# Rotary part of the attention scores as two fp32r products with query and key split into high and low parts

## The chip, the cores and the metric

The kernel runs on one core of a Trainium2 chip. The metric is the device time of one launch in microseconds (us), the median of the runs. The engines of the core are TensorE (PE for its matmuls, PEld for its weight loads), VectorE (DVE), ScalarE (ACT), GpSimd (POOL) and the queue of SyncE (SP), which issues nearly all transfers. Each engine works through its own list of instructions in the order in which the build put them there.

## The reference

One decoder layer: a feed-forward half step, a mixing step in which a gated recurrence (HGRN2) and multi-head latent attention stand beside one another, another feed-forward half step, a gated embedding and a last norm; 512 positions, width 1024. The part that matters is the attention's score, a sum of a part without position (128 columns a head) and a rotary part (64 columns, whose key is the same for all four heads):

```python
q = (rms_norm(cq, q_a_norm[i]) @ w_q_up[i]).reshape(B, S, MLA_HEADS, QK_DIM)
q_nope, q_rope = jnp.split(q, [NOPE_DIM], axis=-1)            # 128 and 64 columns
q_rope = apply_rope(q_rope, cos[:, :, None, :], sin[:, :, None, :])
k_rope = apply_rope(kr, cos, sin)                             # one key for all heads
qf = jnp.concatenate([q_nope, q_rope], axis=-1)
kf = jnp.concatenate([k_nope, k_rope broadcast over the heads], axis=-1)
s = einsum('bhqd,bhkd->bhqk', q[:, :, lo:hi], k[:, :, :hi]) * scale   # 128 queries, keys up to them
```

## The kernel before

Large matmuls run as three fp32r products: each operand is split into a high part (ScalarE copies it to the type fp32r) and a low part (VectorE subtracts the high part from it), and `mm3` adds high·high, high·low and low·high (lines 226 to 230). Products on activations, the attention's scores among them, run as plain fp32, which the trace shows as two matmul instructions each.

Weights come in pieces of 512 KB through seven raw buffers; SP issues a load (line 63) as soon as VectorE has made the low part of the piece whose buffer it takes (lines 73 and 74 make the parts).

Before the attention, `up_projections` makes for each head the queries `qn`, then for each pair of heads the raw rotary queries `qr` in a PSUM bank (heads one above the other, 64 rows each), then four keys `kn`, then four value blocks `vm`. All of these products go through the three PSUM banks with the tag `acc`, in turn, so a bank is taken again by the third next product and must have been copied out by then: `kn` by VectorE (line 826), `qn` and `vm` by ScalarE.

`rope` (line 670) rotates a pair of heads: ScalarE copies the bank to `rpa`, four DMAs on SP's queue bring its rows, with halves exchanged, to `rpb`, VectorE multiplies `rpa` by the cosines and `rpb` by the sines, and two additions of 64 rows each write the two heads' `qr`. Each `qr` has 128 rows, half of them zeros that GpSimd set long before (line 818). The rotary key `krope` holds the 64 key rows twice, one above the other, so that a head's rows meet the key and the other half of the product adds zeros.

`attend` (line 846) takes, for each head, four blocks of 128 queries with 128, 256, 384 and 512 keys: a score bank is the sum of an fp32 product of `kn` and `qn` (line 852) and one of `krope` and `qr` (line 853). Mask, maximum, exponential, normalisation, transposes and the product with `vm` (line 875) follow. `weave` puts steps of the values' projection `uv` and of the recurrence's output `oh` between these steps.

Code order is not the whole order: the framework schedules the instructions of each engine when the kernel is built, and what stands in an engine's list is then fixed.

Of the kernel before, what the change touches and what calls it, by code (L numbers as in the profile page):

```python
# [10 lines left out]
F32 = mybir.dt.float32  # L11
F32R = mybir.dt.float32r
I32 = mybir.dt.int32
U8 = mybir.dt.uint8
AF = mybir.ActivationFunctionType
ALU = mybir.AluOpType
# [147 lines left out]
def block_kernel(ctx: ExitStack, tc: tile.TileContext, xT, pT, pos, wst, items, vecs, lnf, cmask, tmask, out):  # L164
    nc = tc.nc
    V, S, G, PE = nc.vector, nc.scalar, nc.gpsimd, nc.tensor
# [9 lines left out]
    def nm(s):  # L176
        count[0] += 1
        return f"{s}_{count[0]}"

    def slot(name, dt=F32):  # L180
        return slots.tile([P, T], dt, tag="slot", name=nm(name), bufs=NSLOT)
# [50 lines left out]
    def split(src, hi, lo, g=None):  # L232

        if g is None:
            S.activation(hi, src, AF.Copy)  # L235
            V.tensor_tensor(lo, src, hi.bitcast(F32), op=ALU.subtract)  # L236
        else:
            S.activation(hi, src, AF.Copy, scale=g)
            V.scalar_tensor_tensor(lo, src, g, hi.bitcast(F32), op0=ALU.mult, op1=ALU.subtract)
# [373 lines left out]
    kvs = {}  # L613

    def lora():

        us = [acc("uc") for _ in range(3)] + [tps("uc")]
        for k in range(KD):
            w_hi, w_lo = W.next(4)
            for tb in range(4):  # L620
                ts = slice(tb * P, (tb + 1) * P)
                mm3(us[tb][:, :448], (nmix.hi[k][:, ts], nmix.lo[k][:, ts]), (w_hi[:, :448], w_lo[:, :448]),
                    k == 0, k == KD - 1)
                if tb % 2:
                    yield
        kr = slot("kr").rearrange("p (j w) -> p j w", j=4)
        cs = [slot("c") for _ in range(4)]
        ss = tmp.tile([P, 8], F32, tag="css", name="css", bufs=1)
        for tb in range(4):
            S.activation(cs[tb][:, :384], us[tb][:, :384], AF.Copy, scale=rc[:, tb:tb + 1])  # L630
            S.activation(kr[:, tb, :64], us[tb][:, 384:448], AF.Copy, scale=rc[:, tb:tb + 1])
        for tb in range(4):
            sq = tmpt("sq", tag="sq", bufs=2)
            S.activation(sq[:, :256], cs[tb][:, :256], AF.Square, accum_out=ss[:, tb:tb + 1])
            S.activation(sq[:, 256:384], cs[tb][:, 256:384], AF.Square, accum_out=ss[:, 4 + tb:5 + tb])
        yield
        r = rsqrt_of(ss, 8, (256, 128))
        for tb in range(4):
            V.tensor_scalar(cs[tb][:, :256], cs[tb][:, :256], r[:, tb:tb + 1], None, op0=ALU.mult)
            V.tensor_scalar(cs[tb][:, 256:384], cs[tb][:, 256:384], r[:, 4 + tb:5 + tb], None, op0=ALU.mult)  # L640
        yield
        for j, gcol in enumerate((V_QAN, V_QAN + 1, V_KVAN)):
            tp = aux("cT")
            for tb in range(4):
                PE.transpose(tp[:, tb * P:(tb + 1) * P], cs[tb][:, j * P:(j + 1) * P], ident)
            hi, lo = slot("ch", F32R), slot("cl", F32R)
            split(tp, hi, lo, vcol(gcol))
            xc.append((hi, lo))
            yield
        tp = aux("csT")  # L650
        for i, t in enumerate((cos, sin)):
            for tb in range(4):
                o = (i * 4 + tb) * 64
                PE.transpose(tp[:, o:o + 64], t[:64, tb * P:(tb + 1) * P], ident[:64, :64])
        a, b = (tmpt("kra").rearrange("p (j w) -> p j w", j=4) for _ in range(2))
        c4, s4 = (tp[:, i * 256:(i + 1) * 256].rearrange("p (j w) -> p j w", j=4) for i in range(2))
        V.tensor_tensor(a[:, :, :64], kr[:, :, :64], c4, op=ALU.mult)
        for i in range(2):
            o, n = slice(i * 32, (i + 1) * 32), slice(32 - i * 32, 64 - i * 32)
            V.tensor_tensor(b[:, :, o], kr[:, :, n], s4[:, :, o], op=ALU.mult)  # L660
        for i in range(2):
            V.tensor_tensor(kr[:, :, i * 64:(i + 1) * 64], a[:, :, :64], b[:, :, :64], op=ALU.add)
        tp = aux("krT")
        for tb in range(4):
            PE.transpose(tp[:, tb * P:(tb + 1) * P], kr[:, tb, :], ident)
        kvs["rope"] = slot("krope")
        S.activation(kvs["rope"], tp, AF.Copy)
        yield

    def rope(u, outs):  # L670

        a, b = tmpt("rpa"), tmpt("rpb")
        S.activation(a, u, AF.Copy)
        for s in range(4):
            d = s ^ 1
            nc.sync.dma_start(b[d * 32:(d + 1) * 32, :], a[s * 32:(s + 1) * 32, :])
        V.tensor_tensor(a, a, cos, op=ALU.mult)
        V.tensor_tensor(b, b, sin, op=ALU.mult)
        for i, t in enumerate(outs):
            rows = slice(i * 64, i * 64 + 64)  # L680
            V.tensor_tensor(t[rows], a[rows], b[rows], op=ALU.add)

    def chain(*gens):
        for g in gens:
# [116 lines left out]
    qn, qr, kn, vm = [], [], [], []  # L801

    def up_projections():
        for hd in range(H):
            u = acc("qn")
            for j in range(2):
                mm3(u, W.next(), xc[j], j == 0, j == 1)
            t = slot("qn")
            S.activation(t, u, AF.Copy)
            qn.append(t)  # L810
            yield
        for pr in range(2):
            u = acc("qr")
            for j in range(2):
                mm3(u, W.next(), xc[j], j == 0, j == 1)
            ts = [slot("qr") for _ in range(2)]
            for i, t in enumerate(ts):
                G.memset(t[64 - i * 64:128 - i * 64], 0.0)
            rope(u, ts)
            qr.extend(ts)  # L820
            yield
        for hd in range(H):
            u = acc("kn")
            mm3(u, W.next(), xc[2], True, True)
            t = slot("kn")
            V.tensor_copy(t, u)
            kn.append(t)
            yield
        w = W.next(4)
        for j in range(4):  # L830
            u = acc("vm")
            ts = slice(j * P, (j + 1) * P)
            mm3(u, (xc[2][0][:, ts], xc[2][1][:, ts]), w, True, True)
            t = slot("vm")
            S.activation(t, u, AF.Copy)
            vm.append(t)
            yield
# [3 lines left out]
    krope = kvs["rope"]  # L841
# [4 lines left out]
    def attend(hd):  # L846
        pt = [slot("pt") for _ in range(4)]
        for i in range(4):
            n = (i + 1) * P
            qs_ = slice(i * P, n)  # L850
            s = tps("sc")
            PE.matmul(s[:, :n], qn[hd][:, qs_], kn[hd][:, :n], start=True, stop=False)
            PE.matmul(s[:, :n], qr[hd][:, qs_], krope[:, :n], start=False, stop=True)
            V.tensor_tensor(s[:, qs_], s[:, qs_], cm, op=ALU.add)
            mxr = tmp.tile([P, 1], F32, tag="mx", name=nm("mx"), bufs=4)
            V.reduce_max(mxr, s[:, :n], axis=mybir.AxisListType.X)
            V.tensor_scalar(mxr, mxr, -QK_SCALE, None, op0=ALU.mult)
            pr = slot("pr")
            sm = tmp.tile([P, 1], F32, tag="sm", name=nm("sm"), bufs=4)
            S.activation(pr[:, :n], s[:, :n], AF.Exp, bias=mxr, scale=QK_SCALE, accum_out=sm)  # L860
            V.reciprocal(sm, sm)
            V.tensor_scalar(pr[:, :n], pr[:, :n], sm, None, op0=ALU.mult)
            yield
            tp = aux("tp")
            for j in range(i + 1):
                PE.transpose(tp[:, j * P:(j + 1) * P], pr[:, j * P:(j + 1) * P], ident)
            for j in range(i + 1):
                if j % 2:
                    V.tensor_copy(pt[j][:, qs_], tp[:, j * P:(j + 1) * P])
                else:  # L870
                    S.activation(pt[j][:, qs_], tp[:, j * P:(j + 1) * P], AF.Copy)
            yield
        o = aux("om")
        for j in range(4):
            PE.matmul(o[:, j * P:], vm[j][:, hd * P:(hd + 1) * P], pt[j][:, j * P:], start=(j == 0), stop=(j == 3))
        hi, lo = slot("mh", F32R), slot("ml", F32R)
        S.activation(hi, o, AF.Copy)
        V.tensor_tensor(lo, o, hi.bitcast(F32), op=ALU.subtract)
        mla.append((hi, lo))
# [78 lines left out]
    for j in range(2):  # L958
        praw = aslot("praw")
        nc.sync.dma_start(praw, pT[j * P:(j + 1) * P, :])  # L960
        hi, lo = aslot("ph", F32R), aslot("pl", F32R)
# [54 lines left out]
    for tbs in ((0, 1), (2,), (3,)):  # L1016
        for d in range(2):
            us, pjs = [acc("pg") for _ in tbs], [tps("pj") for _ in tbs]
            for k in range(KD):
                if k == 5 and (0, d) not in hT:  # L1020
                    transpose_h(d)
                for u, tb in zip(us, tbs):
                    x_hi, x_lo = n3.x(k)
                    ts = slice(tb * P, (tb + 1) * P)
                    mm3(u, (x_hi[:, ts], x_lo[:, ts]), w_ple(d, k), k == 0, k == KD - 1)
            for k in range(2):
                for pj, tb in zip(pjs, tbs):
                    ts = slice(tb * P, (tb + 1) * P)
# [155 lines left out]
```

## Time and profile before

| what | value |
|---|---|
| median of the runs | 1016.76 us (1016.27 to 1016.96, 3 runs) |
| profiled execution, its own time | 1018.14 us |
| span of its trace | 1016.4 us |
| PE busy | 1003.9 us |
| DVE busy | 746.8 us |
| ACT busy | 458.1 us |
| mean granted TensorE clock | 0.997 of full speed |

The span runs from the first to the last instruction of the trace. Busy times of engines overlap. Matmuls are pipelined and the end of one is modelled, so the length of a matmul step is read from the start of one to the start of the next. All times below are us from the span's start.

### The profile page before, as it was taken

The page shows a single profiled execution, that of the slowest core. Times are in us where ns is not written, and L with a number is a line of the kernel's source. Part 1 is how long each engine was busy: PE and PEld are TensorE (multiplying, and loading weights), DVE is VectorE, ACT ScalarE, POOL GpSimd, SP SyncE. Part 2 cuts the span into 40 slices and gives each one's busy share as a digit, 9 for nine tenths or more (in the row PEclk, how much of TensorE's full clock was granted, in tenths as well). Part 3 has the DMA queues.
Part 4 walks back from the last instruction along what each step waited for, and adds up shares of the span by engine and source line. Part 5 has one row for each costly group of instructions (what it writes and reads, how often), then busy time and mean ns, then how long its engine had stood idle before and what let it go on. Part 6 is the DMA issues. An engine that isn't in the chain of part 4 may idle for free.

```text
span 1016.4 us, 15166 instructions
## 1 busy us (share of the span) xinstructions
PE 1003.9 (99%) x6131; PEld 889.0 (87%) x6131; DVE 746.8 (73%) x1203; ACT 458.1 (45%) x706; POOL 4.6 (0%) x13
## 2 busy tenths in 40 slices
PE   9999999999999999999999999999999999999996
PEld 7899998899998888887777789999988999988885
DVE  7989974579867668765757797898745689766655
ACT  8455541245544341345544545555512355543443
POOL 0000000000000000000000000000000000000000
PEclk9999999999999999999999999999999999999998
DMA  8222344133353321122310221332422223442301
GB/s 308 69 83 85 109 150 124 48 87 121 103 151 122 102 85 64 52 83 67 100 63 1 84 63 42 125 104 84 166 92 75 83 83 105 144 142 89 104 21 63
DMA packets 28982, 97.70 MB, mean 96 GB/s; under 512 B 3456, under 2 KB 3456, under 8 KB 28912
## 3 DMA queue, kind: packets, MB, share of 16 engines
q1 hardware_dynamic: 28752, 96.25, 29.0%
q8 instruction: 48, 0.79, 0.3%
q0 software_dynamic: 160, 0.49, 0.2%
q14 instruction: 22, 0.18, 0.1%
HBM read 94.10 MB, written 2.10 MB: 95 GB/s over the span
## 4 chain that ended last, share of the span: by engine, by line
PE 98%; DVE 1%; ACT 1%; issue 0%; DVEq 0%
PE down L228 8%; PE down L230 8%; PE down L229 8%; PE a L386 7%; PE a L385 7%; PE a L384 7%; PE c L384 4%; PE c L386 4%; PE c L385 4%; PE gu L228 2%; PE gu L229 2%; PE gu L230 2%; PE b L386 2%; PE b L385 2%; PE b L384 2%; PE ufq L228 2%
## 5 line engine op out<-in xcount | busy, mean ns | idle before, releaser
L73 ACT ACTIVATE whi<-wraw 128x1024 fp32r<-128x1024 f32 (+1 forms) x226 | 236.6, 1047 | 378.3 <-PE a L385 92.1
L74 DVE TENSOR_TENSOR wlo<-wraw,whi 128x1024 fp32r<-128x1024 f32 (+1 forms) x226 | 272.2, 1204 | 81.3 <-ACT whi L73 80.2
L229 PE MATMUL down<-al,whi 128*128 128x512 f32 x352 | 137.1, 390 | 0.0
L228 PE MATMUL down<-ah,whi 128*128 128x512 f32 x352 | 137.1, 390 | 0.0
L230 PE MATMUL down<-ah,wlo 128*128 128x512 f32 x352 | 137.0, 389 | 0.0
L384 PE MATMUL c<-sx,whi 128*128 128x256 f32 x304 | 87.9, 289 | 0.8 <-DVE u L418 0.8
L386 PE MATMUL a<-x,wlo 128*128 128x256 f32 x304 | 86.0, 283 | 0.0
L386 PE MATMUL a<-sx,wlo 128*128 128x256 f32 x304 | 86.0, 283 | 0.0
L385 PE MATMUL a<-sx,whi 128*128 128x256 f32 x304 | 86.0, 283 | 0.0
L385 PE MATMUL a<-x,whi 128*128 128x256 f32 x304 | 86.0, 283 | 0.0
L384 PE MATMUL a<-sx,whi 128*128 128x256 f32 x304 | 86.0, 283 | 0.0
L386 PE MATMUL c<-sx,wlo 128*128 128x256 f32 x304 | 86.0, 283 | 0.0
L385 PE MATMUL c<-sx,whi 128*128 128x256 f32 x304 | 86.0, 283 | 0.0
L384 PE MATMUL a<-x,whi 128*128 128x256 f32 x304 | 86.0, 283 | 0.0
L228 PEld LDWEIGHTS down<-ah,whi 128*128 128x128 f32 x352 | 66.1, 188 | 14.1 <-ACT ah L235 0.7
L229 PEld LDWEIGHTS down<-al,whi 128*128 128x128 f32 x352 | 66.1, 188 | 13.9 <-DVE al L236 0.4
L230 PEld LDWEIGHTS down<-ah,wlo 128*128 128x128 f32 x352 | 66.1, 188 | 13.6
L384 PEld LDWEIGHTS c<-sx,whi 128*128 128x128 f32 x304 | 58.1, 191 | 3.6 <-DVE u L418 2.9
L385 PEld LDWEIGHTS a<-x,whi 128*128 128x128 f32 x304 | 58.4, 192 | 0.1
L384 PEld LDWEIGHTS a<-x,whi 128*128 128x128 f32 x304 | 58.4, 192 | 0.1
L385 PEld LDWEIGHTS a<-sx,whi 128*128 128x128 f32 x304 | 58.4, 192 | 0.1
L384 PEld LDWEIGHTS a<-sx,whi 128*128 128x128 f32 x304 | 58.4, 192 | 0.1
(308 smaller groups left out, 2158.9 us busy)
## 6 DMA issues: line engine op xcount, KB each, us to landing
wraw<-wst SPq DMA_DIRECT2D x169, 512.0 KB, 3.4
h<-xT SPq DMA_DIRECT2D x8, 256.0 KB, 6.5
out<-y SPq DMA_DIRECT2D x8, 256.0 KB, 2.2
wraw<-wst SPq DMA_DIRECT2D x7, 256.0 KB, 2.7
rpb<-rpa SPq DMA_DIRECT2D x8, 64.0 KB, 2.2
praw<-pT SPq DMA_DIRECT2D x2, 256.0 KB, 3.1
gf<-lnf SPq DMA_DIRECT2D x2, 256.0 KB, 4.3
posi<-pos POOLq DMA_DIRECT2D x1, 256.0 KB, 4.3
```

Source lines behind the costliest of these rows:

```text
L73: self.nc.scalar.activation(hi, src, AF.Copy)
L74: self.nc.vector.tensor_tensor(lo, src, hi.bitcast(F32), op=ALU.subtract)
L228: PE.matmul(out, a[0], b[0], start=start, stop=False)
L229: PE.matmul(out, a[0], b[1], start=False, stop=False)
L230: PE.matmul(out, a[1], b[0], start=False, stop=stop)
L384: PE.matmul(o, hi[:, c], x[0], start=begin and i == 0 and k == 0, stop=False, skip_group_check=True)
L385: PE.matmul(o, hi[:, c], x[1], start=False, stop=False, skip_group_check=True)
L386: PE.matmul(o, lo[:, c], x[0], start=False, stop=end and i == 1 and k == 3, skip_group_check=True)
```

## The change

The rotated query is kept as fp32r: each head's `qr` holds the high part in rows 0 to 63 and the low part in rows 64 to 127. The rotary keys are split into `krh` and `krl`, both with the 64 rows twice. A score block adds `qr` times `krh` and `qr` times `krl`, which are all four products of the parts. The parts are written by one addition of 128 rows, one split, and then four DMAs per pair of heads that bring the 64-row halves to their places.

```diff
-        kvs["rope"] = slot("krope")
-        S.activation(kvs["rope"], tp, AF.Copy)
+        kvs["rope"] = slot("krh", F32R), slot("krl", F32R)
+        split(tp, *kvs["rope"])
...
         V.tensor_tensor(a, a, cos, op=ALU.mult)
         V.tensor_tensor(b, b, sin, op=ALU.mult)
+        V.tensor_tensor(a, a, b, op=ALU.add)
+        hi, lo = (slot("qrs", F32R) for _ in range(2))
+        split(a, hi, lo)
         for i, t in enumerate(outs):
-            rows = slice(i * 64, i * 64 + 64)
-            V.tensor_tensor(t[rows], a[rows], b[rows], op=ALU.add)
+            for j, part in enumerate((hi, lo)):
+                nc.sync.dma_start(t[j * 64:j * 64 + 64].bitcast(F32), part[i * 64:i * 64 + 64].bitcast(F32))
...
-            ts = [slot("qr") for _ in range(2)]
-            for i, t in enumerate(ts):
-                G.memset(t[64 - i * 64:128 - i * 64], 0.0)
+            ts = [slot("qr", F32R) for _ in range(2)]
             rope(u, ts)
...
-            PE.matmul(s[:, :n], qr[hd][:, qs_], krope[:, :n], start=False, stop=True)
+            for j, part in enumerate(krope):
+                PE.matmul(s[:, :n], qr[hd][:, qs_], part[:, :n], start=False, stop=j == 1)
```

`split` is the function of before: `S.activation(hi, src, AF.Copy)` and then `V.tensor_tensor(lo, src, hi, op=subtract)`.

The lists of the engines change too. On DVE, at the end of the up-projections, this stood before (`kn` is a head's key, `rpa` and `rpb` the two factors of a rotation, `q_324` and `k_302` operands of the recurrence):

```order
L826 COPY kn_399_4665<-kn_398_4661 128x512
L721 TENSOR_TENSOR q_324_4084<-q_324_4084,tots_323_4083 128x2x128
L722 TENSOR_TENSOR k_302_3969<-k_302_3969,tots_323_4083 128x2x128
L826 COPY kn_402_4678<-kn_401_4674 128x512
L826 COPY kn_404_4684<-kn_403_4680 128x512
L826 COPY kn_406_4690<-kn_405_4686 128x512
L74 TENSOR_TENSOR wlo115_4700<-wraw97_4697,whi115_4699 128x1024
L677 TENSOR_TENSOR rpa_391_4628<-rpa_391_4628,cos_1609 128x512
L678 TENSOR_TENSOR rpb_392_4629<-rpb_392_4629,sin_1620 128x512
L681 TENSOR_TENSOR qr_389_4624<-rpa_391_4628,rpb_392_4629 64x512
L681 TENSOR_TENSOR qr_390_4625<-rpa_391_4628,rpb_392_4629 64x512
```

And in the changed kernel, at the same place (line 679 is the addition of 128 rows, line 236 the low part of a split, line 827 the copy of `kn`):

```order
L724 TENSOR_TENSOR q_324_4084<-q_324_4084,tots_323_4083 128x2x128
L725 TENSOR_TENSOR k_302_3969<-k_302_3969,tots_323_4083 128x2x128
L677 TENSOR_TENSOR rpa_392_4628<-rpa_392_4628,cos_1609 128x512
L678 TENSOR_TENSOR rpb_393_4629<-rpb_393_4629,sin_1620 128x512
L679 TENSOR_TENSOR rpa_392_4628<-rpa_392_4628,rpb_393_4629 128x512
L236 TENSOR_TENSOR qrs_395_4639<-rpa_392_4628,qrs_394_4638 128x512
L677 TENSOR_TENSOR rpa_399_4655<-rpa_399_4655,cos_1609 128x512
L678 TENSOR_TENSOR rpb_400_4656<-rpb_400_4656,sin_1620 128x512
L679 TENSOR_TENSOR rpa_399_4655<-rpa_399_4655,rpb_400_4656 128x512
L236 TENSOR_TENSOR qrs_402_4666<-rpa_399_4655,qrs_401_4665 128x512
L827 COPY kn_404_4677<-kn_403_4673 128x512
L827 COPY kn_407_4690<-kn_406_4686 128x512
```

Both rotations, with their splits, have moved ahead of all four copies of `kn`; before, the copies came first.

On PE the changed kernel has this at the same place (`kn_403`, `kn_406`, `kn_408` and `kn_410` are the banks of the four heads' keys, `sc_412` and `sc_420` products of the recurrence, `vm_414` the first value block):

```order
L228 MATMUL kn_408_4692<-ch_352_4317,whi112_4512 128x512 [waits Activation_49]
L229 MATMUL kn_408_4692<-cl_353_4318,whi112_4512 128x512
L230 MATMUL kn_408_4692<-ch_352_4317,wlo112_4513 128x512
L769 MATMUL sc_412_4704<-q_315_4036,k_286_3804 128x256 [waits DVE_49,PE_49]
L770 MATMUL sc_412_4704<-q_315_4036,k_286_3804 128x256
L769 MATMUL sc_420_4733<-q_324_4084,k_302_3969 128x256 [waits DVE_49,PE_49]
L770 MATMUL sc_420_4733<-q_324_4084,k_302_3969 128x256
L228 MATMUL kn_410_4698<-ch_352_4317,whi112_4512 128x512 [waits DVE_49]
L229 MATMUL kn_410_4698<-cl_353_4318,whi112_4512 128x512
L230 MATMUL kn_410_4698<-ch_352_4317,wlo112_4513 128x512
L228 MATMUL vm_414_4715<-whi113_4557,ch_352_4317 128x512 [waits DVE_49]
```

Before, the fourth key product came directly behind the third, one recurrence product behind the fourth, and the other one three value blocks later; now both recurrence products stand ahead of the fourth key product.

On SP's queue the eight new transfers stand between the last `rpb` transfer and the next weight load, in the changed kernel:

```order
L676 DMA rpb_400_4656<-rpa_399_4655 32x512 [waits DMAHW7_49]
L684 DMA qr_390_4626<-qrs_394_4638 64x512 [waits DMAHW0_49,PE_49,Activation_49]
L684 DMA qr_390_4626<-qrs_395_4639 64x512 [waits DMAHW1_49,DVE_49]
L684 DMA qr_391_4627<-qrs_394_4638 64x512 [waits DMAHW2_49]
L684 DMA qr_391_4627<-qrs_395_4639 64x512 [waits DMAHW3_49]
L684 DMA qr_397_4653<-qrs_401_4665 64x512 [waits DMAHW4_49,Activation_49]
L684 DMA qr_397_4653<-qrs_402_4666 64x512 [waits DMAHW5_49,DVE_49]
L684 DMA qr_398_4654<-qrs_401_4665 64x512 [waits DMAHW6_49,PE_49]
L684 DMA qr_398_4654<-qrs_402_4666 64x512 [waits DMAHW7_49]
L63 DMA wraw104_5473<-wst 128x1024 [waits DMAHW0_49,DVE_49]
```

Before, that weight load followed the last `rpb` transfer at once.

## Rows read from the trace of the kernel before

**Rows 1.** The page: the chain that ended last, by engine.
```profile
PE 98%; DVE 1%; ACT 1%; issue 0%; DVEq 0%
```
**Rows 2.** A stretch of the attention: length, then PE, PEld, DVE, ACT, POOL busy, clock.
```profile
524.00:552.00 28.00, 27.21 (x158) 20.69 (x156) 18.30 (x76) 15.67 (x65) 0.00 (x0) 1.00 0.06 20
```
**Rows 3.** PE's timeline, fp32 score products: start, length, line, operands.
```profile
489.49 0.38 PE L852 MATMUL sc<-kn,qn 128*128 128x128 f32 x2
489.71 0.39 PE L853 MATMUL sc<-krope,qr 128*128 128x128 f32 x2
...
502.62 1.02 PE L852 MATMUL sc<-kn,qn 128*128 128x512 f32 x2
503.48 1.02 PE L853 MATMUL sc<-krope,qr 128*128 128x512 f32 x2
```
**Rows 4.** PE's timeline, fp32r products of 512 and of 256 columns.
```profile
300.12 0.39 PE L228 MATMUL down<-ah,whi 128*128 128x512 f32 x1
300.35 0.39 PE L229 MATMUL down<-al,whi 128*128 128x512 f32 x1
...
302.04 0.28 PE L385 MATMUL c<-sx,whi 128*128 128x256 f32 x1
302.16 0.28 PE L386 MATMUL c<-sx,wlo 128*128 128x256 f32 x1
```
**Rows 5.** PE's timeline, fourth key product and an fp32 recurrence product of 256 columns.
```profile
484.30 0.39 PE L228 MATMUL kn<-ch,whi 128*128 128x512 f32 x1
...
484.98 0.59 PE L766 MATMUL sc<-q,k 128*128 128x256 f32 x2
485.41 0.59 PE L767 MATMUL sc<-q,k 128*128 128x256 f32 x2
```
**Rows 6.** DVE's timeline, 482 to 490.
```profile
482.68 0.69 DVE L826 COPY kn<-kn 128x512 f32<-128x512 f32 x1 [1.52 <-PE kn L230]
...
487.18 0.68 DVE L677 TENSOR_TENSOR rpa<-rpa,cos 128x512 f32<-128x512 f32 x1
487.79 0.69 DVE L678 TENSOR_TENSOR rpb<-rpb,sin 128x512 f32<-128x512 f32 x1
488.51 1.41 DVE L681 TENSOR_TENSOR qr<-rpa,rpb 64x512 f32<-64x512 f32 x2
```
**Rows 7.** SP's timeline (last five of eight rotation transfers), and times to landing of all.
```profile
483.51 3.12 SPq L676 DMA_DIRECT2D rpb<-rpa  x5
...
DMA to landing us min/median/max: 2.0/2.2/3.5
```
**Rows 8.** ACT's and DVE's timeline, one split of 128x512, DVE waiting for ACT.
```profile
510.83 0.60 ACT L877 ACTIVATE mh<-om 128x512 fp32r<-128x512 f32 x1 [1.54 <-PE om L875]
...
511.46 0.69 DVE L878 TENSOR_TENSOR ml<-om,mh 128x512 fp32r<-128x512 f32 x1 [1.46 <-ACT mh L877]
```
**Rows 9.** DVE's timeline just behind the rotary key's transposes.
```profile
463.44 1.01 DVE L610 TENSOR_SCALAR gg<-gg,vec 128x512 f32<-128x512 f32 x2 [1.40 <-ACT gg L609]
```
**Rows 10.** PE's timeline at the start: first matmuls, and where their spacing changes.
```profile
1.19 4.21 PE L211 MATMUL idle<-ones_r 128*128 128x512 f32 x9 [1.19 <-DVE ones_r L208]
6.00 0.79 PE L228 MATMUL gu<-x,whi 128*128 128x512 f32 x1 [0.61 <-ACT whi L73]
...
9.16 0.60 PE L229 MATMUL gu<-x,whi 128*128 128x512 f32 x1
9.58 0.41 PE L230 MATMUL gu<-x,wlo 128*128 128x512 f32 x1
9.83 0.40 PE L228 MATMUL gu<-x,whi 128*128 128x512 f32 x1
```
**Rows 11.** PE's last matmul, and stretches behind it (columns as in rows 2).
```profile
1006.93 0.39 PE L230 MATMUL pj<-kh,pl 128*128 128x512 f32 x1
...
1008.00:1010.00 2.00, 0.00 (x0) 0.00 (x0) 1.45 (x7) 0.91 (x4) 0.00 (x0) 0.93 0.00 0
1010.00:1012.00 2.00, 0.00 (x0) 0.00 (x0) 1.65 (x12) 0.14 (x1) 0.00 (x0) 0.50 0.01 4
```

## Prediction

> **What bounds the kernel now.** I read the chain that ended last first: PE holds 98% of it [rows 1], so PE's list of instructions sets the time, and what shortens or interrupts that list is nearly all that counts. Then the stretches of the attention: of the 28 us from 524 to 552 PE is idle 28.00 - 27.21 = 0.8 [rows 2], and before that, from 470 on, its matmuls follow one another without a gap worth naming. So time taken out of PE there is a gain, and a wait put into PE's list is a loss that nothing later gives back. Then PE's timeline for the price of the score products [rows 3 to 5], and last the timelines of DVE, SP and ACT around 480 to 490 [rows 6 to 8], because the order of the lists changes exactly there.
>
> **What is taken off PE.** The length of a step is read from start to start. An fp32 product takes 503.48 - 502.62 = 0.86 us for 512 columns, 0.22 for 128 [rows 3], 0.43 for 256 [rows 5]; 384 columns I put between, at 0.65. An fp32r product takes 0.23 for 512 and 0.12 for 256 columns [rows 4]; 384 by interpolation 0.175. Two of these replace one of those: 0.86 - 0.46 = 0.40 saved at 512, 0.65 - 0.35 = 0.30 at 384, 0.43 - 0.24 = 0.19 at 256. No fp32r product of 128 columns stands in the trace. Its floor is half of that of 256 columns, 0.06, its ceiling one instruction of the fp32 pair, 0.11 [rows 3], so a block of 128 saves 0 to 0.10. I take 0, since the 128-column instructions that are there all take about 0.11. A head saves 0.89 and the four save 3.6 us (4.0 at most).
>
> Not all of it is kept. For heads 0 and 1 the products of `uv` stand between the steps and PE has no gap, so I count their 1.8 in full. For heads 2 and 3 PE already waits now and then, 0.8 us in all [rows 2], for chains of softmax steps that stay as long as they were; what PE saves ahead of such a wait only lengthens the wait. There I keep 1.2, between 0 and 1.8. **Kept: 3.0 us**, bounds 1.8 and 4.0.
>
> **What is hidden.** The split of the key adds one DVE subtraction of 0.69 [rows 8], near 462. DVE stands idle 1.40 there ahead of the `gg` products [rows 9]; without that cover it would cost 0.7. The four memsets on GpSimd go and cost nothing now, since they run long before. The eight new transfers hold SP's queue, and the next weight load is behind them; but that load also needs the buffer that VectorE frees with the low part of weight piece 115, which comes later than the transfers in the new DVE list, so SP would wait anyway.
>
> **The new wait.** This is the largest term. In the new DVE list both rotations with their splits stand ahead of the four copies of `kn`. The PSUM banks of `acc` are three: the fourth key product takes the bank of the first key, so PE can start it only when DVE has copied the first `kn`. Before, that copy started at 482.68, at once behind its product [rows 6]. Now:
>
> - PE is through with the third key product at 484.30 [rows 5]. The two recurrence products that now stand ahead of the fourth take 4 x 0.43 = 1.7. PE is free at **486.0** and stands at the fourth key product; behind it in its list are the value blocks, the first scores and `uv`.
> - DVE starts the first rotation when its fourth transfer has landed: issued at 483.51, landing after 2.2 [rows 7], so 485.7. The two products and the addition start 0.61 and 0.72 apart [rows 6] and the addition of 128 rows takes 0.68, the price of the product of that size: ready at 485.7 + 0.61 + 0.72 + 0.68 = 487.7. ACT makes the high part, 0.60, DVE the low part, 0.69, with 0.03 for each hand-over [rows 8]: 489.0. ACT is free, as its work on the recurrence products ends near 486.7.
> - The second rotation's last transfer is issued near 486.0 and lands near 488.3, so DVE need not wait for it: the same 3.3 us again bring it to 492.4. The copy of the first `kn`, 0.69 [rows 6], ends at **493.1**.
>
> PE stands still for 493.1 - 486.0 = **7.1 us**. Bounds: with the quickest landing, 2.0, it is 6.9; with the slowest, 3.5, for the first rotation, 8.4. After that the DVE copies come every 0.7 us, as quickly as PE takes banks, so no further wait follows. The new transfers of `qr` start at 488.4 (first high part), and at 0.6 each on SP's queue the two of head 0 land by about 491.5; PE has one key and four value products, 5 x 0.69 = 3.4 us, to do from 493.1 before it wants them at 496.5. They are covered by 5 us.
>
> **What the standstill does to the clock.** Before, PE never paused in the middle. The end of the trace shows what a pause does: the last matmul starts at 1006.93, the mean granted clock of 1008 to 1010 is 0.93 and that of 1010 to 1012 is 0.50 [rows 11], so the clock fell to 1.2 GHz near 1009.7, under 3 us after PE's last work. A pause of 7 us is long enough. After it PE runs at half speed until the clock rises. How long, only the start shows: matmuls of 512 columns stand 0.42 apart until 9.58 and then 0.25 and less, from a first matmul at 1.19 with one short gap before 6.00 [rows 10]. From 6.00 that is 3.6 us, from 1.19 without the gap 7.8 us, and half of such a stretch is lost: 1.8 to 3.9. I take the middle, **2.9 us**. If the clock does not fall, this term is 0.
>
> The Trainium skill says the same of the clock ("TensorE: Matmul & The Clock Gate", section "HAM oscillation — how this bites in real kernels"): low speed is the state at rest, and matmuls behind a long wait start slow again. By that rule the sum is the one here; by a trace that only shows full speed in mid-kernel, it is the first rival. The trace's last rows agree with it (0.50 behind the last matmul); no row of before shows a pause in mid-kernel.
>
> **The sum.** +7.1 + 2.9 - 3.0 = **+7.0 us**. The profiled execution took 1018.14, with a span of 1016.4 and 1.7 around it; the changed one would have a span near 1023.4 and take 1025.1. That execution lies 1.4 above the median, so the forecast for the median is 1016.76 + 7.0 = **1023.8 us**.
>
> **The rivals.**
> - *PE stops, but the clock stays up.* Then +7.1 - 3.0 = +4.1: 1020.9. For it: no pause of this length in mid-kernel is on record. Against it: the fall within 3 us at the end.
> - *PE does not stop* (the other side). The passes are saved and the rotations are through before PE wants the bank: 1016.76 - 3.0 = 1013.8, at best 1012.8. It decides at 486.0: the first `kn` copy would have to be done by then. DVE's list would need the eight rotation steps done by 485.3, and the first rotation's data land at 485.7. Only if the wait at the fourth key product were for something else could this hold. A wait of 3 us without a fall of the clock would end level with before, 1016.8.
> - *The new transfers are late as well.* SP issues them one after the other, each with its own wait; if those of head 0 landed 9 us later than I think, past their cover of 5, PE would wait a second time behind the value blocks, at low clock, some 4 us more: 1028. Against it: nothing else moves on that queue at the time, and such transfers now land in 2.0 to 3.5 [rows 7].
> - *The change is made but fp32r products with 128 rows of parts cost what fp32 does.* Then nothing is saved: +10.0, 1026.8. Against it: every `mm3` product in the trace is of that kind and takes 0.23 [rows 4].
>
> **How the numbers follow.** Forecast (stop and clock) 0.70, by its bounds 1016.76 + 6.9 + 1.8 - 4.0 = 1021.5 to 1016.76 + 8.4 + 3.9 - 1.8 = 1027.3; stop without the clock 0.15; no stop 0.05 and level 0.03; late transfers 0.04; nothing saved 0.03. The range runs from 1020.0, below the stop without the clock, to 1027.5. A difference within 0.2%, 2 us, is about what a measurement of this kernel cannot tell from no change. Faster by more 0.05, within 0.04, slower by more 0.91.
>
> **What will show it.** In the changed profile PE must have one idle stretch of about 7 us that begins near 486 and ends with the fourth `kn` product, released by DVE's `kn` copy; the granted clock there must be below 1, and products of 512 columns behind it 0.43 apart for some us. The score products with `krh` and `krl` should be 0.46 apart as a pair of 512 columns and 0.24 at 256. The time from the end of the values' products to the end of the kernel should be as before. I am wrong if DVE's `kn` copies come before the second rotation, if PE's idle time sits elsewhere, or if the 128-column passes take a different time than 0.11.

## The result and the profile after

The changed kernel takes 1023.23 us (median of 6 runs, 1022.85 to 1025.46); before, run beside it, takes 1016.78 (6 runs). The ratio is 1.0063, 95% interval [1.0053, 1.0074]: 6.45 us slower. The profiled execution has a span of 1023.6 us against 1016.4 and a mean granted clock of 0.994 against 0.997.

Executions of one kernel differ by some 2 us here (the two traces of the changed kernel by 2.2, of which 1.7 lie ahead of the attention, where TensorE's first 512-column products come to full speed near 10.4 us in one and before 6.4 in the other), so the parts below are read inside one trace, from a matmul near the start of the attention to the last one.

The page's chain that ended last, which was 98% PE [rows 1], is now 95% PE with 2% of DVE:

```profile
PE 95%; DVE 2%; ACT 1%; issue 0%; DMA 0%; SPq 0%; DVEq 0%
```

PE's waits from 470 to 570 of the changed kernel (us in total, times, longest):

```profile
PE kn L228 <- DVE kn L827: 7.0, 1, 7.0
PE oT L932 <- DVE on L926: 0.7, 1, 0.7
PE om L877 <- ACT pt L873: 0.6, 2, 0.4
```

The last of these stood in before as well, once:

```profile
PE om L875 <- ACT pt L871: 0.4, 1, 0.4
```

One wait is new and large: a key product waits for DVE's copy of a key. PE's timeline around it, at the first score block with 512 keys (answers to [rows 3]), at the end of `uv`, and at the last matmul (answers to [rows 11]):

```profile
486.00 0.59 PE L770 MATMUL sc<-q,k 128*128 128x256 f32 x2
493.62 0.80 PE L228 MATMUL kn<-ch,whi 128*128 128x512 f32 x1 [7.02 <-DVE kn L827]
494.21 0.63 PE L229 MATMUL kn<-cl,whi 128*128 128x512 f32 x1
...
499.45 0.38 PE L853 MATMUL sc<-kn,qn 128*128 128x128 f32 x2
499.59 0.31 PE L855 MATMUL sc<-krh,qr 128*128 128x128 f32 x1
499.73 0.27 PE L855 MATMUL sc<-krl,qr 128*128 128x128 f32 x1
499.85 0.44 PE L228 MATMUL uv<-whi,x 128*128 128x512 f32 x1
500.13 0.39 PE L229 MATMUL uv<-wlo,x 128*128 128x512 f32 x1
...
512.34 1.02 PE L853 MATMUL sc<-kn,qn 128*128 128x512 f32 x2
512.80 0.80 PE L855 MATMUL sc<-krh,qr 128*128 128x512 f32 x1
513.43 0.40 PE L855 MATMUL sc<-krl,qr 128*128 128x512 f32 x1
513.66 0.39 PE L228 MATMUL uv<-whi,x 128*128 128x512 f32 x1
513.90 0.39 PE L229 MATMUL uv<-wlo,x 128*128 128x512 f32 x1
...
533.77 0.38 PE L853 MATMUL sc<-kn,qn 128*128 128x128 f32 x2
...
1014.15 0.39 PE L230 MATMUL pj<-kh,pl 128*128 128x512 f32 x1
```

For the comparison, PE's timeline of the kernel before at the instructions behind the first block of 128 keys, behind the first block of 512 keys, and behind the end of `uv`:

```profile
489.85 0.48 PE L228 MATMUL uv<-whi,x 128*128 128x512 f32 x1
490.17 0.39 PE L229 MATMUL uv<-wlo,x 128*128 128x512 f32 x1
...
503.94 0.79 PE L228 MATMUL uv<-whi,x 128*128 128x512 f32 x1
504.57 0.40 PE L229 MATMUL uv<-wlo,x 128*128 128x512 f32 x1
...
525.04 0.38 PE L852 MATMUL sc<-kn,qn 128*128 128x128 f32 x2
```

What releases the key product is in DVE's timeline: two rotations with a split each, and only then copies of `kn` (answers to [rows 6]):

```profile
486.23 0.69 DVE L677 TENSOR_TENSOR rpa<-rpa,cos 128x512 f32<-128x512 f32 x1 [1.94 <-DMA rpb<-rpa]
...
488.95 0.69 DVE L236 TENSOR_TENSOR qrs<-rpa,qrs 128x512 fp32r<-128x512 f32 x1 [0.70 <-ACT qrs L235]
489.56 0.69 DVE L677 TENSOR_TENSOR rpa<-rpa,cos 128x512 f32<-128x512 f32 x1
...
492.27 0.69 DVE L236 TENSOR_TENSOR qrs<-rpa,qrs 128x512 fp32r<-128x512 f32 x1 [0.69 <-ACT qrs L235]
492.88 1.28 DVE L827 COPY kn<-kn 128x512 f32<-128x512 f32 x2
```

SP's queue holds the transfers (answers to [rows 7]):

```profile
482.02 5.05 SPq L676 DMA_DIRECT2D rpb<-rpa  x8
488.94 5.78 SPq L684 DMA_DIRECT2D qr<-qrs  x8
497.22 0.34 SPq L63 DMA_DIRECT2D wraw<-wst  x1
```

And the stretches from 488 to 500 (columns as in [rows 2]; the granted clock is the third number from the end):

```profile
488.00:490.00 2.00, 0.00 (x0) 0.00 (x0) 1.30 (x3) 0.63 (x1) 0.00 (x0) 1.00 0.01 3
490.00:492.00 2.00, 0.00 (x0) 0.00 (x0) 1.54 (x3) 0.40 (x1) 0.00 (x0) 0.93 0.83 188
492.00:494.00 2.00, 0.38 (x1) 0.39 (x2) 1.73 (x3) 0.23 (x1) 0.00 (x0) 0.50 0.62 141
...
496.00:498.00 2.00, 2.00 (x6) 1.57 (x5) 1.19 (x1) 0.73 (x2) 0.00 (x0) 0.50 0.01 3
498.00:500.00 2.00, 2.00 (x11) 1.67 (x10) 0.00 (x0) 1.41 (x3) 0.00 (x0) 0.86 0.85 270
```

**The time, followed through the two traces.** Each line is the shift of the same point of the program, after minus before:

| point | before | after | shift | what came in between |
|---|---|---|---|---|
| end of the third key product | 484.30 | 484.71 | 0.41 | nearly all of it at the start, where full speed came 0.8 later |
| first `uv` product | 489.85 | 499.85 | 10.00 | stop 7.19, low clock 2.40 |
| score product behind the last `uv` | 525.04 | 533.77 | 8.73 | 1.27 given back |
| last matmul | 1006.93 | 1014.15 | 7.22 | 1.51 given back |

484.71 is 486.00 + 0.43, the end of the recurrence products, less their 4 x 0.43. The stop runs from 486.43 to 493.62. The 15 matmuls from there to 499.45 take 5.83 us; at 0.23 each [rows 4] they would take 3.4. From the end of the third key product to the start of the fourth there are 8.91 us, the stop and the 1.72 of the recurrence products. Without the 0.41 of the start the kernel lost 6.8 us by its own edits.

### The profile page after: what moved, and what is told of

Same layout as the page of the kernel before. It is cut to its first block, busy times and chain, and to the rows that moved or that the text cites. A ratio compares the mean times of both kernels' runs of the same rounds, so it can differ in the third digit from the quotient of the medians.

```text
span 1023.6 us, 15183 instructions
## 1 busy us (share of the span) xinstructions
PE 1003.6 (98%) x6131; PEld 890.4 (87%) x6131; DVE 748.0 (73%) x1204; ACT 458.8 (45%) x708; POOL 2.5 (0%) x9
## 4 chain that ended last, share of the span: by engine, by line
PE 95%; DVE 2%; ACT 1%; issue 0%; DMA 0%; SPq 0%; DVEq 0%
PE down L228 8%; PE down L229 8%; PE down L230 8%; PE a L386 7%; PE a L385 7%; PE a L384 7%; PE c L384 4%; PE c L386 4%; PE c L385 4%; PE gu L228 2%; PE gu L230 2%; PE gu L229 2%; PE b L386 2%; PE b L385 2%; PE b L384 2%; PE ufq L228 2%
```

## The experiments

The expectations in us stand on a before of 1016.8; beside the experiments before took 1016.9 to 1018.4, so it is the ratios that are compared.

**qr_first.** The rotary queries' products stand ahead of the `qn` products, in the code and in the order in which the weights come. The rotations then begin earlier than any key.

```diff
         for pr in range(2):
             u = acc("qr") ...; rope(u, ts)
+        for hd in range(H):
+            u = acc("qn") ...          # moved behind the rotary queries
```

> The changed kernel with the two rotary products of a pair of heads moved ahead of the four query products, in code and in the weight stream, so that both rotations can be through before the keys' banks are wanted. Theory (the cost is the wait of the fourth key product for a copy that stands behind both rotations on VectorE, and the low clock after it): the wait goes or is below 1 us, the clock stays up, and only the saving of about 2.8 us is left, so 1014.0 to 1015.0 us. Rival (the cost is the new path of the query itself, its eight transfers on SP's queue with the weight loads behind them): the path is as long as before, so 1020 us or more.

Measured: 1021.02 us against 1017.72, ratio 1.0033 [1.002, 1.0045]. The key product no longer waits, but the time isn't won: the result is near the rival's, though not for its reason. PE's waits in the new order:

```profile
PE qn L228 <- ACT qn L820: 2.9, 1, 2.9
PE sc L769 <- DVE k L725: 1.9, 1, 1.9
```

The banks are now held on ACT's side. Its timeline shows the high part of the second split, and the copies of `qn` only behind it:

```profile
485.94 0.63 ACT L235 ACTIVATE qrs<-rpa 128x512 fp32r<-128x512 f32 x1 [1.14 <-DVE rpa L679]
486.48 1.07 ACT L820 ACTIVATE qn<-qn 128x512 f32<-128x512 f32 x2
```

The clock falls here too. PE's last work ahead of the second wait ends at 484.2, the granted clock is 1.00 from 484 to 486 and 0.51 from 486 to 488, and the 14 products from 487.11 to 493.08 take 5.97 us where 14 x 0.23 would be 3.2. It follows that the 7 us hang on the order of the lists, not on how much work there is: the same work in another order gives two other, smaller waits, one of them for another bank. It doesn't show what the passes are worth.

**before_qr_first.** The same move in the kernel before, which has no splits.

> The kernel before with the same move of the rotary products ahead of the query products: a control. Theory: the move alone is worth nothing, since PE had no wait there, 1016.8 us within 0.7. If the move alone gains, 1015 or less, what the changed kernel with the move shows is not the worth of the two fp32r products.

Measured: 1020.77 us, ratio 1.0025 [1.0016, 1.0035]; the expectation failed. PE's largest wait there:

```profile
PE sc L766 <- DVE k L722: 1.7, 1, 1.7
```

The move alone costs 0.25%, some 2.5 us; 1.7 of them are this wait, since a recurrence product now comes before DVE has its operand, and the rest isn't traced. So the step from qr_first to this kernel says nothing of the splits, and the move was a poor way to take the stop away.

**rotate_late.** `rope` only copies and issues its transfers; VectorE's part, with the splits, is called behind the loop over the four keys.

```diff
-    def rope(u, outs):
+    def rope(u):
         ...
+        return a, b
+    def rotate(a, b, outs):
         V.tensor_tensor(a, a, cos, op=ALU.mult)
...
-            rope(u, ts)
+            ropes.append((*rope(u), ts))
...
+        for r in ropes:                # behind the four keys
+            rotate(*r)
```

> The changed kernel with the VectorE part of the rotations written behind the key products, so that the copies of the keys stand ahead of them. Theory: PE no longer waits at the fourth key product; the queries now come later, and a wait of 0 to 2.5 us for their transfers may stand at the first scores, too short for the clock to fall: 1014 to 1016.8 us. Rival (the transfers bound it): the first scores wait 5 us or more and the time stays at 1020 or above.

Measured: 1017.13 us against 1017.72, ratio 0.9986 [0.9975, 0.9996], mean clock 0.997. DVE's timeline has the copies first again, as in [rows 6]:

```profile
483.20 0.69 DVE L832 COPY kn<-kn 128x512 f32<-128x512 f32 x1 [1.52 <-PE kn L230]
...
484.48 1.92 DVE L832 COPY kn<-kn 128x512 f32<-128x512 f32 x3
...
487.70 0.69 DVE L681 TENSOR_TENSOR rpa<-rpa,cos 128x512 f32<-128x512 f32 x1
```

The stop and the fall of the clock are gone with nothing else of the change undone (PE's list, too, has the recurrence products behind the fourth key product again): the two are what made the kernel slower. It beats the changed kernel by 0.8% and before by 0.14%, 1.4 us with an interval from 0.4 to 2.5. What is left of the late rotation is one short wait of PE, for the last transfers:

```profile
PE sc L862 <- DMA qr<-qrs: 0.8, 1, 0.8
```

**fp32_scores.** The changed kernel with the rotary part of the scores as one plain fp32 product again; the split of the query, the transfers and the layout stay (the query's tiles have the type fp32 again).

```diff
-        kvs["rope"] = slot("krh", F32R), slot("krl", F32R)
-        split(tp, *kvs["rope"])
+        kvs["rope"] = slot("krope")
+        S.activation(kvs["rope"], tp, AF.Copy)
...
-            for j, part in enumerate(krope):
-                PE.matmul(s[:, :n], qr[hd][:, qs_], part[:, :n], start=False, stop=j == 1)
+            PE.matmul(s[:, :n], qr[hd][:, qs_], krope[:, :n], start=False, stop=True)
```

> The changed kernel with one part undone: the rotary query still comes as high and low part through the eight transfers, but the key stays one fp32 tile and a score block has one fp32 product with it, as before. Theory: the wait at the fourth key product and the low clock stay, 7.0 and 2.4 us, and the saving of about 2.8 goes, so 1026 us, within 0.7. Rival (the products save the full 3.6 that their lengths give, and something else costs more than the wait): 1026.8. If the products save nothing: 1023.2.

Measured: 1028.1 us, ratio 1.0096 [1.0082, 1.011]. The stop is the same:

```profile
PE kn L228 <- DVE kn L827: 7.0, 1, 7.0
```

So the stop doesn't hang on the passes, and the two passes give back 0.0033 x 1017 = 3.4 us by the runs' ratios, give or take 1.8 by the two intervals, and 2.5 by the traces (from the first `uc` product to the last matmul 600.1 against 597.6). The ratio alone doesn't tell the expected 2.8 from the rival's 3.6; the traces lie nearer to the first.

**busy_wait.** 26 fp32r products that nobody reads, between the third and the fourth key product in the code, to keep PE at work while it waits.

```diff
+            if hd == 3:
+                for _ in range(26):
+                    PE.matmul(busy, ones_r, ..., start=True, stop=True)
             u = acc("kn")
```

> The changed kernel with 26 fp32r products of 512 columns on a spare bank, whose result nobody reads, put between the third and the fourth key product, about 5.9 us of work at full clock inside the wait of 7.0. Theory: the copy of the first key is as late as before, so the length of the wait with the filling in it is the same, but the clock never falls and its 2.4 us are saved: 1020.8 us, with PE's own wait down to about 1.3 us and the granted clock at 1 throughout. Rival (the slow spell behind the wait costs nothing, because something else would have held the products there): 1023.2.

Measured: 1024.95 us against 1018.44, ratio 1.0068 [1.0054, 1.0082]. In the profiled execution, of 1023.27 us, the clock stayed at full speed, yet no time came back; the median one, of which there is no trace, has a mean clock of 0.995 against its 0.997. The build had put the products ahead of the recurrence products, whose results ACT copies; ACT's timeline shows those copies in front of the second split's high part, which thereby starts later:

```profile
490.73 0.60 ACT L772 ACTIVATE ao<-sc 128x512 f32<-128x512 f32 x1 [2.80 <-PE sc L770]
491.59 0.60 ACT L772 ACTIVATE ao<-sc 128x512 f32<-128x512 f32 x1 [0.27 <-PE sc L770]
492.08 0.62 ACT L235 ACTIVATE qrs<-rpa 128x512 fp32r<-128x512 f32 x1
```

From the end of the third key product to the start of the fourth there are now 10.34 us (483.74 to 494.08), 1.4 more than the 8.91 of the changed kernel. The fill made the stop end later, so this run doesn't price the clock. The next one puts the same products where they delay nothing.

**busy_in_wait.** The 26 products are emitted behind the second recurrence product, so PE's list has them directly ahead of the fourth key product.

```diff
     # behind the last recurrence product of head 3
+        if hd == 3:
+            for _ in range(26):
+                PE.matmul(busy, ones_r, ..., start=True, stop=True)
```

> Twenty-six fp32r products of 512 columns that nobody reads stand on TensorE directly ahead of the fourth key product, behind both recurrence products, so they fill the wait itself and delay nothing that VectorE or ScalarE needs; nothing is left out. Theory (stop plus a low clock behind it): the fourth key product starts when the changed kernel's does, since VectorE's copy of the first key sets that; the granted clock stays at 1.00 from 486 to 500, and the 2.4 us that the low clock cost come back: 1.0063 - 0.0024, about 1.004 of before. Rival (the fill delays the copy again, as in busy_wait, or the clock costs nothing): 1.0063 or more.

Measured: 1021.0 us against 1016.92, ratio 1.0041 [1.0028, 1.0054]. PE's timeline (the dummy products are one row):

```profile
484.26 6.28 PE L774 MATMUL busy<-ones_r 128*128 128x512 f32 x26
491.53 0.50 PE L228 MATMUL kn<-ch,whi 128*128 128x512 f32 x1 [0.99 <-DVE kn L831]
...
495.06 0.38 PE L857 MATMUL sc<-kn,qn 128*128 128x128 f32 x2
```

The stretch in which the clock fell in the changed kernel (the granted clock is the third number from the end):

```profile
490.00:492.00 2.00, 1.01 (x5) 0.54 (x4) 1.82 (x4) 0.15 (x1) 0.00 (x0) 1.00 0.60 138
```

The key product still waits for DVE's copy, so the stop is as long as ever, filled or not: 8.81 us from the end of the third key product (482.72) to the start of the fourth. Behind it the 15 matmuls take 495.06 - 491.53 = 3.53 us, not 5.83.

**after_again.** The changed kernel once more, beside busy_in_wait and late_fp32.

> The changed kernel once more, to stand beside the other two under the same conditions: 1.0063 of before, with the 7 us stop at the fourth key product and the low clock behind it. If the ratio moves by more than 0.001, the sizes of the earlier comparisons carry that much doubt.

Measured: 1023.23 us, ratio 1.0059 [1.0047, 1.0071]. PE's timeline at the stop:

```profile
491.87 0.80 PE L228 MATMUL kn<-ch,whi 128*128 128x512 f32 x1 [6.99 <-DVE kn L827]
...
497.28 0.38 PE L853 MATMUL sc<-kn,qn 128*128 128x128 f32 x2
```

Here the 15 matmuls take 5.41 us. busy_in_wait is 1023.23 - 1021.0 = 2.2 us quicker, give or take 1.8 by the two intervals, and its 15 matmuls 5.41 - 3.53 = 1.9: what the low clock cost came back, and the stop itself stayed.

**late_fp32.** rotate_late with the fp32 product of fp32_scores.

> The kernel of rotate_late (rotation behind the copies of the keys, so no stop) with the score's rotary part as one plain fp32 product again; the split, the transfers and the layout of the query stay, and nothing of the result is left out. Theory (the passes save about 2.5 us of TensorE wherever the stop is): 2.5 us above rotate_late, a ratio near 1.001 to before. Rival (rotate_late gains by its order alone, and the passes only saved time that the changed kernel's stop left over): equal to rotate_late within 0.5 us, 0.9985 to 0.999.

Measured: 1018.24 us against 1016.92, ratio 1.0009 [1.0, 1.0018]. That is 0.0023 above rotate_late, 2.3 us, give or take 1.4 us by the two intervals, as expected; the two traces, from the first `uc` product to the last matmul, differ by only 1.3 (590.8 and 589.5), and some 0.2 of the 2.3 lies outside the spans (2.0 us in late_fp32, 1.8 in rotate_late). PE's waits behind 500 differ in two lines. rotate_late:

```profile
PE c L384 <- DVE u L418: 0.9, 2, 0.7
PE oT L939 <- DVE on L933: 0.7, 1, 0.7
```

late_fp32 has 0.2 for the first and none of the second. The first, late in the kernel, varies from trace to trace with no edit near it (none named in busy_in_wait, 0.3 and 0.4 in the two of the changed kernel, 0.8 in before). The second is the passes' own: it stands at 0.7 in all six traces with fp32r scores (after, after_again, qr_first, busy_wait, busy_in_wait, rotate_late) and in none of the four with fp32 scores (before, before_qr_first, fp32_scores, late_fp32).

## Why the prediction was right, step by step

The forecast was 1023.8 us (1020.0 to 1027.5); measured 1023.23. By terms:

| step | predicted | measured | where |
|---|---|---|---|
| stop at the fourth key product | 7.1 (6.9 to 8.4) | 7.19 | 486.43 to 493.62, released by DVE's `kn` copy |
| low clock behind it | 2.9 (1.8 to 3.9) | 2.4, 2.0 in after_again | 15 matmuls in 5.83 and 5.41 us |
| passes, kept | 3.0 (1.8 to 4.0) | 2.8 (1.27 + 1.51) | the table of shifts |
| sum | +7.0 | +6.8 in the traces, +6.45 by the medians | |

**The stop** came where the lists said and for the reason given. The chain behind it ran as costed: rotation data landed for 486.2 (predicted 485.7; 0.41 of the difference is this trace's late start), 3.3 us from each rotation's start to the next work (486.23 to 489.56 and to 492.88), the copy of the first `kn` behind the second split. rotate_late shows the cause: with the copies first, nothing stops. The rival "no stop" is refuted for the change as made, and realised by that kernel; but it gives 1.4 us (0.4 to 2.5) and not the 3.0 of that rival. The passes keep 2.8, with a new wait of 0.7 for `on` already counted, and a wait of 0.8 for `qr` comes in; what is left of the difference is inside the interval.

**The clock** fell as forecast, though later than the end of before suggested: granted 1.00 from 488 to 490 and 0.93 from 490 to 492, so it changed to the lower level (1.2 GHz) near 491.7, 5.3 us after PE's last work, where before's last matmul was followed by the fall within 3 [rows 11]; in after_again, with 0.77 from 488 to 490, it was 4.4 us. It was back at 2.4 GHz near 498.5. The size, 2.4 and 2.0 against 2.9, is off inside its bounds: the start of the kernel was a rough measure of it. The rival "PE stops, but the clock stays up" was put at 1020.9; busy_in_wait makes that kernel, at 1021.0 (1020.9 by its ratio). The rule of the Trainium skill ("TensorE: Matmul & The Clock Gate", "HAM oscillation — how this bites in real kernels"), that matmuls behind a long wait start slow again, agrees with the 0.50 from 492 to 498.

**The passes** have the prices that were forecast, if a group is read to the second instruction behind it. A step behind an fp32 product is recorded as starting early (0.46 behind `kn` times `qn` where the next is fp32r, 0.86 where it is fp32), and the rest shows in the next row. From the score's first product to the second `uv` product the 512-key block takes 504.57 - 502.62 = 1.95 before [rows 3] and 513.90 - 512.34 = 1.56 after: 0.39 saved, 0.40 forecast. The 128-key block takes 490.17 - 489.49 = 0.68 and 500.13 - 499.45 = 0.68: nothing saved, as forecast, so the two passes of 128 columns take 0.68 - 0.22 - 0.23 = 0.23, 0.11 each. What the prediction said would show these steps, pairs 0.46 and 0.24 apart, was badly chosen for that reason: the pair of 512 reads 0.63 + 0.23, and the saving is there all the same. Another of its signs didn't fit its own sum: the time behind the values' products was to be as before, though 1.2 us were to be kept there.

What was kept is divided otherwise than forecast. Heads 0 and 1 keep 1.27, not their 1.8 in full: `uv` doesn't cover every chain. PE is idle for 0.29 us between the first `uv` product and the score product behind the last (33.92 long, 33.63 busy), before for 0.01 (35.19 and 35.18); 0.2 of that is a new wait for ACT's copy of `pt`, at 517.7, ahead of head 0's product with the values (in the list of waits 0.6 for `om` in two places, against 0.4 in one before). The idle time makes 0.3 of the 0.5 that is missing; the other 0.2 isn't traced to a row. Behind `uv`, 1.51 comes back against 1.2 forecast: PE's busy time up to the last matmul falls by 1.83 (480.24 to 478.41) and its idle time grows by 0.32 (1.65 to 1.97). There the new wait of 0.7 for `on` takes its part of the 1.8, about as forecast, and the wait of line 384, which no edit touches, happened to be 0.3 instead of 0.8. That the total of the passes is right is partly luck, because these two errors are of opposite sign.

**What was called hidden** was hidden. The key's split, near 462, costs PE nothing: from 420 to 500 PE's list of waits has the stop alone. SP issues the eight `qr` transfers by 494.7 and the next weight load follows at 497.22; PE's first use of `qr` at 499.59 waits for nothing. The rivals "late transfers" and "fp32r costs as fp32" are refuted by that row and by fp32_scores (2.5 us slower).

Of the experiments' own expectations three failed, those of qr_first, before_qr_first and busy_wait, the last in its time though not in the clock of its trace: each time the move took one wait away and the build's order of the lists made another that had not been looked for.

## What to carry to other kernels

Before counting what a change saves on the busiest engine, read the new order of every list that hands back its buffers: work that is free by its duration can stand in front of a copy that frees a bank, and here 7 us of that, and 2 us of low clock behind it, outweighed 3 us of faster matmuls. The remedy is to put the slow chain behind the copies, not to start it earlier; the version with the rotation behind the keys beats both kernels at 0.9986 of before, and a fill that keeps the clock up is worth only the clock's share of the loss. Price a matmul by whole groups up to the second instruction behind them, because a step next to an fp32 product shows part of its time in the row of its successor.

## What the runs showed of the hardware that was not expected

The start of an fp32r matmul behind an fp32 one is recorded 0.40 us early at 512 columns (0.46 after the fp32 start, then a step of 0.63 where 0.23 is usual), and the sum of the two is 1.09 = 0.86 + 0.23. The clock fell 5.3 us after PE's last work in the middle of the changed kernel, 4.4 in after_again, 1.9 in qr_first, where PE had also waited 1.9 just before, and within 3 at the end of before, so one fall was no measure of the other; in busy_wait's trace a wait of 2.5 left it at 1.00. And 26 products whose results nobody reads held the clock at 1.00 through the same wait.
